# A two-layer decoder trunk: attention in calls of four heads, the first block's scores as one matmul over both key parts, sinks as a column behind the scores, the division on VectorE

## Chip, cores and metric

One core of a Trainium2 chip. The time is device microseconds of one execution, the median of three: 1176.08 us for the kernel before (1176.0 to 1176.14). Five engines work in it, each through its own queue in order: TensorE (PE in the profile; PEld its weight loads), VectorE (DVE), ScalarE (ACT), GpSimd (POOL) and SyncE (SP), which here only issues DMAs.

## What is computed

Two layers on 256 rows of 1024 floats. A layer is a half-step SwiGLU FFN, a mixing sub-layer and a second FFN, each with RMS norms before and behind it. The change lies in one branch of the mixing sub-layer, attention over a sliding window:

```python
def sliding_window_attention(q, k, v, sinks):
    # 16 query heads of 64, 2 key heads; blocks of 128 rows; a block sees itself and the one before
    scores = jnp.einsum('bnqgrd,bnkgd->bngrqk', qb, k2) * scale
    scores = jnp.where(valid[None, :, None, None], scores, MASK_VALUE)
    m = jnp.maximum(scores.max(axis=-1), sink)
    p = jnp.exp(scores - m[..., None])
    probs = p / (p.sum(axis=-1) + jnp.exp(sink - m))[..., None]
    out = jnp.einsum('bngrqk,bnkgd->bnqgrd', probs, v2)
```

The first block of 128 rows has nothing before it, so its scores have 128 columns; the second block's have 256. The sink is one more logit per head: it enters the maximum and the sum, and has no value.

The mixing sub-layer has a second branch (a gated unit, "gating"), two sigmoid gates and an output projection.

## The kernel before

**Precision.** Each fp32 operand is split into a high and a low part that the matmul unit takes at its faster fp32 rate: ScalarE casts the high part (`high`, L143, for weights; L206 for activations), VectorE subtracts to get the low part (L152, L207). A product is then three matmuls: high by high, high by low, low by high. For the scores the query's two parts are kept stacked, so two matmuls do: one with the keys' high part (`kth`, L766), one with their low part (`ktl`, L767).

**Weights.** They stream from HBM in units of 512 KB through four raw buffers and nine split buffers. After the product of a unit the program splits further units up to seven ahead (`AHEAD`, in `upto`).

**Order.** The program fixes the order of every engine's queue itself (`manual_schedule`); the framework puts in the waits that data and reused buffers need. In the middle of the mixing sub-layer TensorE goes through 48 products, one per weight unit: 8 for the gated unit's input (0 to 7), 8 for the queries (8 to 15), then the gate b (16 to 23), the gated unit's branch (24 to 31), the gate a (32 to 39) and the attention's branch (40 to 47). `beside` runs each product and puts other work ahead of it and behind it. A place is a half-step: 2c is ahead of product c, 2c + 1 behind it; 2c + 1 and 2c + 2 follow each other with no product between, only the split of the next weight unit.

**Attention** (`attend`) is a generator that is resumed at half-steps counted from its start: scores on TensorE at 0; at +3 VectorE adds the mask, takes the maximum with the sink as starting value (one instruction per head, L773), and negates it (L777); at +4 ScalarE exponentiates each head with that bias and sums the row (L786); at +7 VectorE takes the reciprocal of the sum plus the sink's exponential (L779, L788, L791, L793) and GpSimd multiplies (L794); at +11 TensorE transposes the probabilities (L803), ScalarE and VectorE split them; at +16 the value products (L815, L816); at +18 to +21 ScalarE copies one half of the partitions over (L826), VectorE adds the two halves ("sides", L829), and the result is split (L832, L834). `ATTEND` holds the half-steps at which the calls start. There are six calls per layer: for each key head, all eight heads of the first block in one call, then the second block in two calls of four heads.

**What else is at those places.** Query evacuations (L917, L920) up to product 16, copies of finished gate products (L935), and at product 31 the sigmoid of gate b on ScalarE (L945), for which ScalarE loads another table, and its product on GpSimd (L948).

**Buffers.** TensorE's results go to eight PSUM banks in turn (`mm`); the 512-wide temporaries to six buffers (`t2`), the probabilities to two (`t4`). Which buffer is given next, and so whom the next writer waits for, is fixed when the program is built.

Of the kernel before, what the change touches and what calls it, by code (L numbers as in the profile page):

```python
# [30 lines left out]
NKV = 2  # L31
HD = 64
# [21 lines left out]

WARM = (11, 6)

ATTEND = (27, 32, 38, 44, 50, 56)
GATING = (9, 10, 11, 12)

GATE = (31, 33)  # L60
# [3 lines left out]
def trunk(ctx: ExitStack, tc: tile.TileContext, a: dict, out: bass.AP):  # L64
    nc = tc.nc

    def pool(name, bufs, **kw):
        return ctx.enter_context(tc.tile_pool(name=name, bufs=bufs, **kw))

    const = pool("const", 1)  # L70
# [5 lines left out]
    t4 = pool("t4", 2)  # L76
    t2 = pool("t2", 6)
    kvp = pool("kv", 1)
# [3 lines left out]
    tiny2 = pool("tiny2", 2)  # L82
# [122 lines left out]
    def split(h, lo, src):  # L205
        nc.scalar.copy(h, src)  # L206
        nc.vector.tensor_tensor(out=lo, in0=src, in1=f(h), op=ALU.subtract)  # L207
# [40 lines left out]
    def bank():  # L248
        return new(mm, [P, 512], "mm")
# [401 lines left out]
    class FFN:  # L651
# [10 lines left out]
        def prepare(self):  # L662
            self.into = [(new(m8, [P, 8, S], "m8", F32R), new(m8, [P, 8, S], "m8", F32R))]
# [27 lines left out]
    class Mix:  # L691
# [29 lines left out]
        def prepare(self):  # L721
            vs = new(n8, [P, NT, D], "n8")
            vv = new(kvp, [P, NT, NKV, 2, HD], "vv", F32R)
            kth = new(kvp, [P, NKV, S], "kth", F32R)
# [25 lines left out]
        def attend(self, g, n, heads):  # L750


            _, vv, kth, ktl = self.into[:4]
            l, qs_, yah, yal = self.l, self.qs, self.yah, self.yal
            nh = len(heads)
            order = heads[0::2] + heads[1::2]
            nk = (n + 1) * P
            qs = rows_of(n)
            half = nh // 2
            s = [bank().rearrange("p (a b) -> p a b", a=half) for _ in range(2)]  # L760
            for i in range(half):
                for r in range(2):


                    q_ = qs_[r][:, heads[0] // 2 + i, qs]
                    nc.tensor.matmul(s[r][:, i, :], q_, kth[:, g, 0:nk], start=True, stop=False)  # L766
                    nc.tensor.matmul(s[r][:, i, :], q_, ktl[r][:, g, 0:nk], start=False, stop=True)  # L767
            yield 3
            m = new(tiny2, [P, 8], "m")
            p = new(t4, [P, nh, nk], "t4")  # L770
            mk = mask.rearrange("p a b -> p (a b)")[:, 256 - nk:]
            for i, hd in enumerate(order):
                nc.vector.tensor_tensor_reduce(out=p[:, i, :], in0=s[i // half][:, i % half, :], in1=mk, scale=1.0,  # L773
                                               scalar=sinks[:, l, hd:hd + 1], op0=ALU.add, op1=ALU.max,
                                               accum_out=m[:, i:i + 1])
            nm = new(tiny2, [P, 8], "nm")
            nc.vector.tensor_scalar(out=nm[:, :nh], in0=m[:, :nh], scalar1=-1.0, scalar2=None, op0=ALU.mult)  # L777
            sk = new(tiny2, [P, 8], "sk")
# [5 lines left out]
            sm = new(tiny2, [P, 8], "sm")  # L784
            for i in range(nh):
                nc.scalar.activation(p[:, i, :], p[:, i, :], AF.Exp, bias=nm[:, i:i + 1],  # L786
                                     accum_out=sm[:, i:i + 1])
            nc.scalar.activation(sk[:, :nh], sk[:, :nh], AF.Exp)  # L788
            yield 3
            dn = new(tiny2, [P, 8], "dn")  # L790
            nc.vector.tensor_tensor(out=dn[:, :nh], in0=sm[:, :nh], in1=sk[:, :nh], op=ALU.add)  # L791
            rd = new(tiny2, [P, 8], "rd")
            nc.vector.reciprocal(rd[:, :nh], dn[:, :nh])  # L793
            nc.gpsimd.tensor_tensor(out=p, in0=p, in1=rd[:, :nh].unsqueeze(2).to_broadcast([P, nh, nk]),  # L794
                                    op=ALU.mult)
            yield 4
            parts = []
            for i0 in range(0, nh, 4):

                for c in range(n + 1):  # L800
                    ps = bank()
                    for i, hd in enumerate(range(i0, i0 + 4)):
                        nc.tensor.transpose(ps[:, i * P:(i + 1) * P], p[:, hd, c * P:(c + 1) * P], ident)  # L803
                    ph, pl = new(t2, [P, 512], "t2", F32R), new(t2, [P, 512], "t2", F32R)
                    split(ph, pl, ps)
                    parts.append((i0, c, ph, pl))
            yield 5
            outs = []
            for i0, c, ph, pl in parts:
                if c == 0:  # L810
                    o = bank()
                    outs.append((i0, o.rearrange("p (a b) -> p a b", a=4)))

                v = vv[:, c, g].rearrange("p r d -> p (r d)")
                nc.tensor.matmul(o, v, ph, start=(c == 0), stop=False)  # L815
                nc.tensor.matmul(o, v, pl, start=False, stop=(c == n))  # L816
            yield 2

            y0, y = [new(t2, [P, half, P], "t2") for _ in range(2)]
            sides = []  # L820
            for r in range(2):
                i0, o = outs[r % len(outs)]
                at = r * half - i0
                sides.append((slice(r * HD, (r + 1) * HD), slice((1 - r) * HD, (2 - r) * HD), o[:, at:at + half, :]))
            for own, other, o in sides:
                nc.scalar.copy(y0[own], o[other])  # L826
            yield 1
            for own, other, o in sides:
                nc.vector.tensor_tensor(out=y[own], in0=o[own], in1=y0[own], op=ALU.add)  # L829
            yield 1  # L830
            js = slice(heads[0] // 2, heads[0] // 2 + half)
            nc.scalar.copy(yah[:, js, qs], y)  # L832
            yield 1
            nc.vector.tensor_tensor(out=yal[:, js, qs], in0=y, in1=f(yah[:, js, qs]), op=ALU.subtract)  # L834

        def middle(self, xt, xth, xtl, turn1, early):
# [86 lines left out]
            calls = []  # L923
            for g in range(NKV):
                h0 = g * 8
                calls.append((g, 0, list(range(h0, h0 + 8))))
                for i0 in range(0, 8, 4):
                    calls.append((g, 1, list(range(h0 + i0, h0 + i0 + 4))))
# [63 lines left out]
    ident = new(const, [P, P], "ident")  # L992
# [20 lines left out]
    sinks = new(const, [P, DEPTH, NH], "sinks")  # L1013
# [3 lines left out]
    mask = new(const, [P, 2, P], "mask")  # L1017
# [4 lines left out]
                            base=0, pattern=[[-1, P]], channel_multiplier=1)  # L1022


    ktl = [new(const, [P, NKV, S], f"ktl{r}", F32R) for r in range(2)]
    for k in ktl:
        nc.gpsimd.memset(f(k), 0.0)

# [44 lines left out]
    parts = [new(tiny2, [P, 2], "parts") for _ in range(NT)]  # L1073
# [38 lines left out]
    for i in range(4):  # L1112
# [3 lines left out]
                            in1=g0[:, 4:8].unsqueeze(2).to_broadcast([P, 4, P]), op=ALU.mult)  # L1116
# [129 lines left out]
```

## Time and profile before

| | |
|---|---|
| median of 3 runs | 1176.08 us |
| the profiled execution | 1175.91 us, its span 1174.0 us |
| granted TensorE clock | 0.999 |
| PE, DVE, ACT, POOL busy | 99%, 72%, 58%, 5% of the span |
| GpSimd's divisions (L794) | 12, 26.1 us |
| scores of the first block (L766, L767, 128 columns) | 64 matmuls |

A row of the order of time has start, duration, engine, line, operation, output and inputs, their shapes, and in brackets how long the engine was idle before and who ended that. Durations of matmuls are latencies and overlap; what one costs TensorE is the distance to the next start. A row of the waits has who waited for whom, the total in us, how often, and the longest. A row of the groups has the number of instructions, busy us and mean ns, then idle time ahead of them. A row of the stretches has its bounds, its length, busy us of PE, PEld, DVE, ACT and POOL, then clock, DMA share and GB/s.

### The profile page before, as it was taken

The page shows a single profiled execution, that of the slowest core. Times are in us where ns is not written, and L with a number is a line of the kernel's source. Part 1 is how long each engine was busy: PE and PEld are TensorE (multiplying, and loading weights), DVE is VectorE, ACT ScalarE, POOL GpSimd, SP SyncE. Part 2 cuts the span into 40 slices and gives each one's busy share as a digit, 9 for nine tenths or more (in the row PEclk, how much of TensorE's full clock was granted, in tenths as well). Part 3 has the DMA queues.
Part 4 walks back from the last instruction along what each step waited for, and adds up shares of the span by engine and source line. Part 5 has one row for each costly group of instructions (what it writes and reads, how often), then busy time and mean ns, then how long its engine had stood idle before and what let it go on. Part 6 is the DMA issues. An engine that isn't in the chain of part 4 may idle for free.

```text
span 1174.0 us, 16947 instructions
## 1 busy us (share of the span) xinstructions
PE 1164.8 (99%) x6293; PEld 1006.9 (86%) x6293; DVE 842.6 (72%) x1430; ACT 675.4 (58%) x1147; POOL 58.9 (5%) x43
## 2 busy tenths in 40 slices
PE   9999999999999999999999999999999999999997
PEld 7888888999888888888888888889988888888886
DVE  6767758877787867766676677589778787676752
ACT  6656644657775456555455665455577754555551
POOL 0000000001131000000000000000021220000000
PEclk9999999999999999999999999999999999999999
DMA  7576673645457346557635657745544662565560
GB/s 249 182 255 230 219 250 141 203 168 175 140 175 241 137 142 215 183 198 266 216 108 193 224 193 240 230 141 183 182 169 137 210 225 81 179 200 198 198 210 37
DMA packets 61427, 220.81 MB, mean 188 GB/s; under 512 B 7072, under 2 KB 7072, under 8 KB 61344
## 3 DMA queue, kind: packets, MB, share of 16 engines
q1 hardware_dynamic: 61056, 219.46, 56.1%
q8 instruction: 50, 0.82, 0.3%
q10 hardware_dynamic: 288, 0.27, 0.1%
q14 instruction: 33, 0.27, 0.1%
HBM read 218.65 MB, written 1.05 MB: 187 GB/s over the span
## 4 chain that ended last, share of the span: by engine, by line
PE 99%; ACT 0%; DVE 0%; issue 0%; DVEq 0%; POOL 0%; POOLq 0%
PE mm L289 51%; PE mm L319 34%; PE mm L296 3%; PE mm L297 3%; PE mm L298 3%; PE mm L254 1%; PE mm L803 1%; PE mm L767 1%; PE mm L766 1%; PE mm L736 1%; PE mm L816 0%; PE mm L815 0%; PE mm L1065 0%; PE mm L276 0%; ACT n L1038 0%; ACT t L1113 0%
## 5 line engine op out<-in xcount | busy, mean ns | idle before, releaser
L152 DVE TENSOR_TENSOR wl<-raw,wh 128x1024 fp32r<-128x1024 f32 x370 | 452.7, 1248 | 88.0 <-ACT wh L143 85.9
L143 ACT CAST wh<-raw 128x1024 fp32r<-128x1024 f32 x370 | 381.7, 1052 | 152.9 <-DMA raw<-in_ffn_w 71.4
L289 PE MATMUL mm<-wh,m 128*128 128x512 f32 x1088 | 341.7, 391 | 0.0
L319 PE MATMUL mm<-xt,wh 128*128 128x512 f32 x1152 | 276.6, 391 | 0.0
L319 PEld LDWEIGHTS mm<-xt,wh 128*128 128x128 f32 x1152 | 211.4, 188 | 40.7
L289 PEld LDWEIGHTS mm<-wh,m 128*128 128x128 f32 x1088 | 204.3, 188 | 42.1
L289 PE MATMUL mm<-wl,m 128*128 128x512 f32 x544 | 211.8, 389 | 0.0
L319 PEld LDWEIGHTS mm<-xt,wl 128*128 128x128 f32 x1152 | 147.7, 191 | 5.6
L319 PE MATMUL mm<-xt,wl 128*128 128x256 f32 x1152 | 149.4, 283 | 0.0
L289 PE MATMUL mm<-wh,xt 128*128 128x512 f32 (+1 forms) x480 | 144.1, 378 | 0.0
L681 DVE TENSOR_TENSOR t<-mm,t 128x256 f32<-128x256 f32 x144 | 61.0, 424 | 101.7 <-ACT t L680 101.7
L289 PEld LDWEIGHTS mm<-wl,m 128*128 128x128 f32 x544 | 102.2, 188 | 20.6
L680 ACT COPY t<-mm 128x256 f32<-128x256 f32 x144 | 52.4, 364 | 88.7 <-PE mm L319 88.7
L289 PEld LDWEIGHTS mm<-wh,xt 128*128 128x128 f32 x480 | 88.4, 188 | 16.0
L289 PE MATMUL mm<-wl,xt 128*128 128x512 f32 (+1 forms) x240 | 87.5, 375 | 0.0
L296 PE MATMUL mm<-xt,wh 128*128 128x256 f32 x256 | 73.3, 286 | 0.0
L298 PE MATMUL mm<-xt,wl 128*128 128x256 f32 x256 | 72.4, 283 | 0.0
L297 PE MATMUL mm<-xt,wh 128*128 128x256 f32 x256 | 72.4, 283 | 0.0
L683 ACT ACTIVATE t<-t 128x256 f32<-128x256 f32 x72 | 30.1, 418 | 46.3 <-DVE t L681 46.3
L289 PE MATMUL mm<-m,xt 128*128 128x512 f32 x216 | 54.5, 397 | 0.0
L289 PEld LDWEIGHTS mm<-wl,xt 128*128 128x128 f32 x240 | 45.2, 188 | 7.9
L794 POOL TENSOR_TENSOR t<-t,rd 128x1024 f32<-128x1024 f32 x12 | 26.1, 2171 | 505.8 <-DVE rd L793 488.2
(156 smaller groups left out, 1094.0 us busy)
## 6 DMA issues: line engine op xcount, KB each, us to landing
raw<-in_ffn_w SPq DMA_DIRECT2D x263, 512.0 KB, 4.5
raw<-in_w_in SPq DMA_DIRECT2D x84, 512.0 KB, 4.1
raw<-in_w_sgu_branch SPq DMA_DIRECT2D x16, 512.0 KB, 3.6
raw<-in_w_attn_branch SPq DMA_DIRECT2D x16, 512.0 KB, 3.8
raw<-in_w_out SPq DMA_DIRECT2D x16, 512.0 KB, 4.5
gain<-in_ffn_post_g SPq DMA_DIRECT2D x4, 512.0 KB, 6.4
gain<-in_ffn_pre_g SPq DMA_DIRECT2D x3, 512.0 KB, 6.7
x<-in_x SPq DMA_DIRECT2D x4, 256.0 KB, 4.9
```

Of the source, the lines that this page charges most:

```text
L143: nc.scalar.copy(h, self.raw[u])
L152: nc.vector.tensor_tensor(out=lo, in0=self.raw[u], in1=f(h), op=ALU.subtract)
L254: nc.tensor.transpose(ps[:, k, :], src[:, (c0 + k) * P:(c0 + k + 1) * P], ident)
L289: nc.tensor.matmul(o, every[i][0], every[i][1], start=start and i == 0, stop=stop and i == 2)
L296: nc.tensor.matmul(o, wh[:, ks], ah[:, k, :], start=(k == 0), stop=False)
L297: nc.tensor.matmul(o, wh[:, ks], al[:, k, :], start=False, stop=False)
L298: nc.tensor.matmul(o, wl[:, ks], ah[:, k, :], start=False, stop=(k == KD - 1))
L319: nc.tensor.matmul(out_, w[:, k * P:(k + 1) * P], x, start=(k == 0 and x.shape[1] == 2 * S), stop=(k == KD - 1 and x.shape[1] == 2 * S))
L680: nc.scalar.copy(y[:, half, :], o[half][:, S:2 * S])
L681: nc.vector.tensor_tensor(out=y[:, half, :], in0=o[half][:, 0:S], in1=y[:, half, :], op=ALU.add)
L683: nc.scalar.activation(y[:, 0, :], y[:, 0, :], AF.Silu)
L794: nc.gpsimd.tensor_tensor(out=p, in0=p, in1=rd[:, :nh].unsqueeze(2).to_broadcast([P, nh, nk]), op=ALU.mult)
```

## The change

Attention is called eight times per layer with four heads each, for both blocks. In the first block one matmul of 256 columns goes over the keys' low and high part side by side (`keys`, three planes: low part for the query's upper half, high part, low part for the other half; any two neighbours are one operand); VectorE first adds the mask to one half of the result (L775), and the reduction adds the other half (L779). The sink is copied as one more column behind the scores (L785), so that the exponential's row sum holds it; the small additions and exponentials for it go. VectorE multiplies by the reciprocal (L795) in GpSimd's place. The offsets inside a call stay; the calls start at other half-steps.

```diff
-ATTEND = (27, 32, 38, 44, 50, 56)
+ATTEND = (25, 29, 33, 38, 43, 47, 52, 57)
...
-            s = [bank().rearrange("p (a b) -> p a b", a=half) for _ in range(2)]
-            for i in range(half):
+            s = [bank().rearrange("p (a b) -> p a b", a=2) for _ in range(2)]
+            for i in range(2):
                 for r in range(2):
...
                     q_ = qs_[r][:, heads[0] // 2 + i, qs]
-                    nc.tensor.matmul(s[r][:, i, :], q_, kth[:, g, 0:nk], start=True, stop=False)
-                    nc.tensor.matmul(s[r][:, i, :], q_, ktl[r][:, g, 0:nk], start=False, stop=True)
+                    if n == 0:
+                        nc.tensor.matmul(s[r][:, i, :], q_, keys[:, r:r + 2, g, 0:nk], start=True, stop=True)
+                    else:
+                        nc.tensor.matmul(s[r][:, i, :], q_, kth[:, g, 0:nk], start=True, stop=False)
+                        nc.tensor.matmul(s[r][:, i, :], q_, ktl[r][:, g, 0:nk], start=False, stop=True)
             yield 3
...
+            p = new(t4, [P, 4, nk + 1], "t4")
+            if n == 0:
+                for r in range(2):
+                    nc.vector.tensor_tensor(out=p[:, 2 * r:2 * r + 2, 0:nk], in0=s[r][:, :, 0:nk],
+                                            in1=mask[:, 1:2, :].to_broadcast([P, 2, P]), op=ALU.add)
...
-            nc.vector.tensor_tensor(
-                out=sk[:, :nh].rearrange("p (r j) -> p r j", r=2),
-                in0=sinks[:, l, heads[0]:heads[0] + nh].rearrange("p (j r) -> p r j", r=2),
-                in1=nm[:, :nh].rearrange("p (r j) -> p r j", r=2), op=ALU.add)
+            nc.scalar.copy(p[:, :, nk:nk + 1].rearrange("p (r j) a -> p r (j a)", r=2),
+                           sinks[:, l, heads[0]:heads[0] + 4].rearrange("p (j r) -> p r j", r=2))
             yield 1
...
-            nc.scalar.activation(sk[:, :nh], sk[:, :nh], AF.Exp)
             yield 3
-            nc.vector.tensor_tensor(out=dn[:, :nh], in0=sm[:, :nh], in1=sk[:, :nh], op=ALU.add)
-            nc.vector.reciprocal(rd[:, :nh], dn[:, :nh])
-            nc.gpsimd.tensor_tensor(out=p, in0=p, in1=rd[:, :nh].unsqueeze(2).to_broadcast([P, nh, nk]),
-                                    op=ALU.mult)
+            nc.vector.reciprocal(rd, sm)
+            nc.vector.tensor_tensor(out=p[:, :, 0:nk], in0=p[:, :, 0:nk],
+                                    in1=rd.unsqueeze(2).to_broadcast([P, 4, nk]), op=ALU.mult)
             yield 4
...
+            calls = [(g, n, list(range(h, h + 4))) for g in range(NKV) for n in range(NT)
+                     for h in range(g * 8, g * 8 + 8, 4)]
...
+    keys = new(const, [P, 3, NKV, S], "keys", F32R)
+    kth, ktl = keys[:, 1], (keys[:, 0], keys[:, 2])
```

The calls of a layer are numbered here in the order in which they start: before, 1 and 4 are the eight-head calls; after, 1, 2, 5 and 6 are calls of the first block, 3, 4, 7 and 8 of the second.

VectorE's queue in the first layer, before, from the split of the second call's probabilities to the first call's sides and the next call's reduction (t_592, t_595: that split; wl: a weight's low part; t_604: the sides; mm_3141: scores of the fourth call):

```order
L207 TENSOR_TENSOR t_592_3123<-mm_3117,t_591_3122 128x512
L207 TENSOR_TENSOR t_595_3132<-mm_3126,t_594_3131 128x512
L152 TENSOR_TENSOR wl_3088<-raw_2980,wh_3087 128x1024
L791 TENSOR_TENSOR dn_3171<-sm_3093,sk_3084 128x4
L793 RECIPROCAL rd_3173<-dn_3171 128x4
L152 TENSOR_TENSOR wl_3136<-raw_3004,wh_3135 128x1024
L829 TENSOR_TENSOR t_604_3177<-mm_3111,t_603_3176 64x512
L829 TENSOR_TENSOR t_604_3177<-mm_3114,t_603_3176 64x512
L773 ISA t_609_3201,m_3200<-mm_3141,mask_125,sinks_122 128x128
```

The same place after: the split of call 3 (t_598, t_601), call 1's sides (t_592), call 4's reciprocal and division (t_583), and call 5's mask additions and first reduction (t_608):

```order
L207 TENSOR_TENSOR t_598_3131<-mm_3125,t_597_3130 128x512
L207 TENSOR_TENSOR t_601_3140<-mm_3134,t_600_3139 128x512
L823 TENSOR_TENSOR t_592_3116<-mm_3073,t_591_3115 64x256 x2
L794 RECIPROCAL rd_3160<-sm_3092 128x4
L795 TENSOR_TENSOR t_583_3077<-t_583_3077,rd_3160 128x4x256
L152 TENSOR_TENSOR wl_3120<-raw_3012,wh_3119 128x1024
L775 TENSOR_TENSOR t_608_3171<-mm_3109,mask_125 128x2x128
L775 TENSOR_TENSOR t_608_3171<-mm_3110,mask_125 128x2x128
L779 ISA t_608_3171,m_3170<-mm_3109,t_608_3171,sinks_122 128x128
```

Behind these rows come three more reductions, the negation, a small low part (L828), a weight's low part and call 2's sides (L823). By the wait counts of the built program the second split waits for call 2's first value product (its buffer), and TensorE's transposes of call 4 wait for call 2's sides (their bank).

ScalarE's queue, before, at the last call's exponentials (t_668) and the sigmoid (n_542), with the split of the fifth call's probabilities (t_678, t_681) ahead of the table load:

```order
L786 ACTIVATE t_668_3451,sm_3473<-t_668_3451,nm_3456 128x256 x4
L788 ACTIVATE sk_3458<-sk_3458 128x4
L206 CAST t_678_3496<-mm_3491 128x512
L206 CAST t_681_3505<-mm_3500 128x512
L143 CAST wh_3509<-raw_3392 128x1024
L945 ACT_TABLE_LOAD
L945 ACTIVATE n_542_2914<-n_542_2914 128x2x512
```

After: call 8's exponentials (t_676), the sigmoid (n_541), and then the split of call 7's probabilities (t_686, t_689):

```order
L790 ACTIVATE t_676_3461,sm_3485<-t_676_3461,nm_3466 128x257 x4
L143 CAST wh_3490<-raw_3380 128x1024
L935 ACT_TABLE_LOAD
L935 ACTIVATE n_541_2898<-n_541_2898 128x2x512
L206 CAST t_686_3519<-mm_3514 128x512
L206 CAST t_689_3528<-mm_3523 128x512
```

The casts of the seventh call now stand behind the table load and the sigmoid; before, the casts of the last call but one stood ahead of them.

More of the change, by code (lines that the diff above doesn't have):

```diff
@@ L772, in attend @@
+            yield 3
+            m = new(tiny2, [P, 4], "m")
+            p = new(t4, [P, 4, nk + 1], "t4")
[3 more added lines that the diff above has]
+                                            in1=mask[:, 1:2, :].to_broadcast([P, 2, P]), op=ALU.add)
             for i, hd in enumerate(order):
-                nc.vector.tensor_tensor_reduce(out=p[:, i, :], in0=s[i // half][:, i % half, :], in1=mk, scale=1.0,
-                                               scalar=sinks[:, l, hd:hd + 1], op0=ALU.add, op1=ALU.max,
+                part = s[i // 2][:, i % 2, :]
+                nc.vector.tensor_tensor_reduce(out=p[:, i, 0:nk], in0=part[:, P:2 * P] if n == 0 else part,
+                                               in1=p[:, i, 0:nk] if n == 0 else mask.rearrange("p a b -> p (a b)"),
+                                               scale=1.0, scalar=sinks[:, l, hd:hd + 1], op0=ALU.add, op1=ALU.max,
@@ L775, in attend @@
                                                accum_out=m[:, i:i + 1])
[L776 to L782 removed]
+            nm = new(tiny2, [P, 4], "nm")
@@ L783, in attend @@
+            nc.vector.tensor_scalar(out=nm, in0=m, scalar1=-1.0, scalar2=None, op0=ALU.mult)
+            nc.scalar.copy(p[:, :, nk:nk + 1].rearrange("p (r j) a -> p r (j a)", r=2),
+                           sinks[:, l, heads[0]:heads[0] + 4].rearrange("p (j r) -> p r j", r=2))
             yield 1
-            sm = new(tiny2, [P, 8], "sm")
-            for i in range(nh):
+            sm = new(tiny2, [P, 4], "sm")
+            for i in range(4):
                 nc.scalar.activation(p[:, i, :], p[:, i, :], AF.Exp, bias=nm[:, i:i + 1],
@@ L807, in attend @@
-            yield 5
[L808 to L812, printed above, removed]
+            for c in range(n + 1):
+                ps = bank()
+                for i in range(4):
+                    nc.tensor.transpose(ps[:, i * P:(i + 1) * P], p[:, i, c * P:(c + 1) * P], ident)
+                ph, pl = new(t2, [P, 512], "t2", F32R), new(t2, [P, 512], "t2", F32R)
+                split(ph, pl, ps)
+                parts.append((c, ph, pl))
@@ L814, in attend @@
+            yield 5
+            o = bank()
+            for c, ph, pl in parts:
                 v = vv[:, c, g].rearrange("p r d -> p (r d)")
@@ L816, in attend @@
                 nc.tensor.matmul(o, v, pl, start=False, stop=(c == n))
+            o = o.rearrange("p (a b) -> p a b", a=4)
             yield 2
[L819 to L824, printed above, removed]
+            y0, y = [new(t2, [P, 2, P], "t2") for _ in range(2)]
+            sides = [(slice(r * HD, (r + 1) * HD), slice((1 - r) * HD, (2 - r) * HD), o[:, 2 * r:2 * r + 2, :])
+                     for r in range(2)]
             for own, other, o in sides:
@@ L830, in attend @@
             yield 1
-            js = slice(heads[0] // 2, heads[0] // 2 + half)
+            js = slice(heads[0] // 2, heads[0] // 2 + 2)
             nc.scalar.copy(yah[:, js, qs], y)
```

24 lines of the change are left out of this document (1 added, 23 removed).

## The prediction

> **What bounds the kernel now.** I read the page's busy times and its chain, then the waits of TensorE (PE), then the busy times by stretch.
>
> ```profile
> span 1174.0 us, 16947 instructions
> PE 1164.8 (99%) x6293; PEld 1006.9 (86%) x6293; DVE 842.6 (72%) x1430; ACT 675.4 (58%) x1147; POOL 58.9 (5%) x43
> PE 99%; ACT 0%; DVE 0%; issue 0%; DVEq 0%; POOL 0%; POOLq 0%
> ```
> ```profile
> PE mm L1065 <- POOL ident masks.py:199: 1.4, 1, 1.4
> PE mm L289 <- ACT n L1038: 0.4, 1, 0.4
> ```
> ```profile
> 306.00:320.00 14.00, 14.00 (x79) 12.07 (x79) 10.56 (x23) 10.98 (x29) 1.90 (x1) 1.00 0.44 136
> ```
>
> The chain that ended last is TensorE alone; its two longest waits of the whole run, shown here, are 1.4 and 0.4 us and lie at the start. In the stretch of the attention that the third view shows, TensorE is busy for 14.00 of 14 us, VectorE for 10.56 and ScalarE for 10.98. So a microsecond taken from TensorE's work is a microsecond of the kernel, and a microsecond that TensorE must wait is one as well. Work on VectorE costs nothing until TensorE reaches something VectorE hasn't finished. Two questions decide: how much matmul time goes, and whether VectorE and ScalarE still keep ahead.
>
> **What TensorE saves.** These are matmuls in order of time; the first column is the start, and what counts is start to start, since each is shown with its latency.
>
> ```profile
> 267.08 0.22 PE L766 MATMUL mm<-kth,m 128*128 128x128 f32 x1
> ...
> 268.82 0.33 PE L296 MATMUL mm<-xt,wh 128*128 128x256 f32 x1
> 268.99 0.28 PE L297 MATMUL mm<-xt,wh 128*128 128x256 f32 x1
> ...
> 274.63 0.28 PE L766 MATMUL mm<-kth,m 128*128 128x256 f32 x1
> ...
> 275.59 0.40 PE L289 MATMUL mm<-wh,xt 128*128 128x512 f32 x1
> ...
> 283.78 0.28 PE L766 MATMUL mm<-kth,m 128*128 128x256 f32 x1
> 284.73 1.03 PE L803 MATMUL mm<-ident,t 128*128 128x128 f32 x8
> 285.52 0.48 PE L289 MATMUL mm<-wh,xt 128*128 128x512 f32 x1
> 285.84 0.40 PE L289 MATMUL mm<-wl,xt 128*128 128x512 f32 x1
> ...
> 293.82 0.39 PE L815 MATMUL mm<-t,vv 128*128 128x512 f32 x1
> 294.73 1.03 PE L803 MATMUL mm<-ident,t 128*128 128x128 f32 x8
> ```
>
> The sixteen 128-column score matmuls of a first-block call, with the longer step behind them, take 268.99 - 267.08 - 0.12 = 1.79 us. Eight of 256 columns take 275.59 - 274.63 = 0.96 us. A layer has two such calls of eight heads: (1.79 - 0.96) x 2 x 2 layers = 3.3 us. The eight transposes cost 285.84 - 284.73 - 0.23 = 0.88 us in one group, and two groups of four (0.36 + 0.09 each) cost 0.89: nothing. The value products stay. [...]
>
> Whether a moving operand in two pieces of 128, as the side-by-side keys are, streams like one of 256 no row shows. Between 0.12 us each (the 256-column rows) and 0.22 (two of 128), I take 0.12, the same column count; at the other end the gain is gone.
>
> **What VectorE and ScalarE take on.** The rows that price it, VectorE first, then ScalarE and GpSimd (POOL):
>
> ```profile
> L681 DVE TENSOR_TENSOR t<-mm,t 128x256 f32<-128x256 f32 x144 | 61.0, 424 | 101.7 <-ACT t L680 101.7
> L143 ACT CAST wh<-raw 128x1024 fp32r<-128x1024 f32 x370 | 381.7, 1052 | 152.9 <-DMA raw<-in_ffn_w 71.4
> ```
> ```profile
> 301.17 0.35 DVE L773 CUSTOM_DVE_ANT_0 t<-mm,mask,sinks 128x128 f32<-128x128 f32 x1
> ...
> 303.46 0.17 DVE L777 TENSOR_SCALAR nm<-m 128x8 f32<-128x8 f32 x1
> ...
> 308.01 1.29 DVE L207 TENSOR_TENSOR t<-mm,t 128x512 fp32r<-128x512 f32 x2 [2.43 <-ACT t L206]
> 309.21 1.22 DVE L152 TENSOR_TENSOR wl<-raw,wh 128x1024 fp32r<-128x1024 f32 x1
> 310.35 0.16 DVE L791 TENSOR_TENSOR dn<-sm,sk 128x8 f32<-128x8 f32 x1
> 310.54 0.20 DVE L793 RECIPROCAL rd<-dn 128x8 f32<-128x8 f32 x1
> 310.70 0.86 DVE L829 TENSOR_TENSOR t<-mm,t 64x256 f32<-64x256 f32 x2
> 311.59 2.30 DVE L152 TENSOR_TENSOR wl<-raw,wh 128x1024 fp32r<-128x1024 f32 x1
> 313.92 0.48 DVE L773 CUSTOM_DVE_ANT_0 t<-mm,mask,sinks 128x256 f32<-128x256 f32 x1
> ...
> 315.67 0.17 DVE L777 TENSOR_SCALAR nm<-m 128x4 f32<-128x4 f32 x1
> ...
> 315.95 0.42 DVE L834 TENSOR_TENSOR m<-t,m 128x256 fp32r<-128x256 f32 x1
> 316.29 1.22 DVE L152 TENSOR_TENSOR wl<-raw,wh 128x1024 fp32r<-128x1024 f32 x1
> ```
> ```profile
> 303.73 0.40 ACT L786 ACTIVATE t<-t,nm 128x128 f32<-128x128 f32 x1 [0.98 <-DVE nm L777]
> ...
> 306.83 0.19 ACT L788 ACTIVATE sk<-sk 128x8 f32<-128x8 f32 x1
> ...
> 307.40 1.06 ACT L206 CAST t<-mm 128x512 fp32r<-128x512 f32 x2
> ...
> 315.93 0.51 ACT L786 ACTIVATE t<-t,nm 128x256 f32<-128x256 f32 x1 [2.93 <-DVE nm L777]
> ...
> 317.92 0.19 ACT L788 ACTIVATE sk<-sk 128x4 f32<-128x4 f32 x1
> ...
> 331.11 1.28 ACT L945 ACT_TABLE_LOAD   x1
> 332.41 1.06 ACT L945 ACTIVATE n<-n 128x1024 f32<-128x1024 f32 x1
> ```
> ```profile
> 310.91 1.90 POOL L794 TENSOR_TENSOR t<-t,rd 128x1024 f32<-128x1024 f32 x1 [9.34 <-DVE rd L793]
> ```
>
> Per layer VectorE gets eight additions of the mask (0.34 to 0.42 each, by L834's spacing and L681) and eight divisions: four of 512 elements (0.6, like L207) and four of 1024 (1.14, a weight's low part, 310.35 - 309.21): 3.2 + 2.4 + 4.6 = 10 us. The small additions that go give back some 2 us. GpSimd's division gives back something too: the low part at 311.59 began while GpSimd's division ran, and ended 1.08 us after that one's end at 312.81, 2.30 us instead of 1.22. [...] That saves 1.1 us where they met. ScalarE's copies of the sinks (0.1 to 0.2 each) replace its small exponentials: nothing. No DMA is added or moved.
>
> What matters is that VectorE's and ScalarE's queues are in order, and each call now makes VectorE reduce, ScalarE exponentiate, and VectorE divide, eight times per layer instead of six. I number the calls 1 to 8 (their half-steps: 25, 29, 33, 38, 43, 47, 52, 57) and price two stretches; a product of 12 matmuls is (283.78 - 275.59) / 3 = 2.73 us.
>
> **First wait, at call 4's transposes.** The second half of call 3's split takes the buffer that call 2's value product reads, so VectorE can't start it before that product. From there TensorE has two value matmuls (0.455), a product (2.73), four scores (0.48), a product (2.73) and four value matmuls (0.91), 7.3 us, until call 4's transposes. Their bank is freed by the addition of call 2's sides (L823). In VectorE's queue that stands behind: the value matmul's end (0.39), split (0.6), call 1's sides (0.89), call 4's reciprocal and division (0.2 + 1.14), a low part (1.14), call 5's mask, maximum and negation (0.8 + 1.15 + 0.2 = about 2.1), a small low part (0.34), a low part (1.14), and itself (0.86): 8.8 us. TensorE waits 1.5 us. Its second group of transposes takes a bank freed by a ScalarE copy behind call 5's exponentials: 6.5 (the sum up to the negation) + 1.55 + 1.05 + 0.6 = 9.7, against 8.8 + 0.4: another 0.5. In the profile the sides of the call before were done at 301 us and their bank taken at 306.5; that cover of 5 us is what the closer calls use up.
>
> **Second wait, at call 8's transposes.** From call 4's second group TensorE has nine products (24.6), sixteen scores (1.92), 0.45 + 0.45 + 0.45 + 0.88 of transposes and 0.91 + 0.455 + 0.455 + 0.91 of value products: 31.4 us. VectorE starts 0.6 later and has six splits (3.6), eight low parts (9.1), one reduction of call 6 (2.1), two of 256 columns (1.92 each), two short and two long divisions (4.4), three small low parts (1.0) and three sums of sides (2.6): 26.7 us. It also waits for ScalarE: 0.8 at call 5's split, 1.5 at call 6's, and 3.9 at call 7's, where the cast stands behind call 8's exponentials (1.99), a weight cast (1.05), the table load (1.28) and the sigmoid (1.0), plus its own 0.6, while VectorE has 2.0 to do. That is 33.5 us, so TensorE waits 2.0.
>
> **The sum.** 4.0 us per layer, both layers being laid out alike: 8.0. The profiled execution took 1175.91 us, its span and 1.9 around it, 0.17 under the median of 1176.08. 1175.9 - 3.3 + 8.0 = 1180.6; with the 0.2 to the median, 1180.8 us. The sums of durations carry about a twentieth: 0.45 of the first stretch and 1.7 of the second, 4.3 us over both layers, so 1176.5 to 1185.
>
> **Rivals.** *VectorE keeps ahead, faster.* If an instruction starts before the one ahead has written (as 309.21 to 310.35 shows, less than its 1.22) more often than I reckon, and the ScalarE waits overlap, both stretches shrink. The point is the first one: at 7.3 us or less there, and 6% off the second, TensorE never waits and the time is 1172.8. For it: VectorE had 3.4 of 14 us free. Against: the order of the queue leaves it no other work to put ahead. *The gain is just eaten.* One of the two stretches is short and the other fits: 1176.1 - 3.3 + 4 = 1176.8, no change. *Worse.* The sigmoid's end lets GpSimd's gate product run into the low part or division ahead of call 8's transposes, and these wait as at 311.59: 1.1 more per layer, 1183.0; with the twentieth on top, over 1185. *The scores don't do what they say*: pieces of 128 at 0.22 us, no gain, 1184; I count it with the last one.
>
> **How the numbers follow.** Forecast 0.57, VectorE ahead 0.15, gain just eaten 0.18, worse 0.10. A measurement of this kernel tells about 0.2%, 2.4 us, from no change. Faster by more holds the first rival and a sliver: 0.16. Within it lie the second rival and the forecast's low edge: 0.22. Slower: 0.62. The range leaves out the worst tenth: 1172.6 to 1185.0; the forecast's own is 1176.5 to 1185.
>
> **What would show it.** L764 at 0.12 us start to start, 32 of them, shows the gain. Among TensorE's waits, new rows for L802 and L289 with VectorE (L823, L779, L795) as releasers, some 4 us per layer, show the loss; with no such rows the second and third steps are wrong. VectorE's wait for the cast behind the sigmoid (L207 on L206, about 4 us) shows the second stretch. The forecast is wrong if TensorE's idle time stays at 2 us, or if its waits fall at products for lack of weights (L152), which I hold to be seven units ahead.

## The result, and the profile after

The changed kernel takes 1186.54 us (median of 5 executions, 1185.36 to 1186.88) against 1176.08 for the kernel before: a ratio of 1.0087, 95% interval 1.0076 to 1.0097. It is slower, as forecast, but by 10.5 us and not by 4.7, and 1186.54 lies above the range (1172.6 to 1185.0). The profiled execution took 1186.32 us.

The page of the changed kernel, its span, its busy times and the shares of the chain that ended last:

```profile
span 1184.3 us, 16899 instructions
PE 1165.6 (98%) x6261; PEld 1003.8 (85%) x6261; DVE 855.2 (72%) x1458; ACT 676.1 (57%) x1163; POOL 33.1 (3%) x31
PE 80%; DVE 11%; ACT 6%; issue 1%; DMA 1%; DVEq 0%; POOL 0%; ACTq 0%; POOLq 0%
```

TensorE was the whole chain before; now VectorE and ScalarE hold 17% of it. TensorE's waits name the places:

```profile
PE mm L802 <- DVE t L795: 5.2, 2, 2.6
PE mm L289 <- DVE m L779: 1.8, 2, 1.0
...
PE mm L802 <- DVE t L823: 1.0, 2, 0.5
PE mm L254 <- DVE t L502: 0.9, 1, 0.9
...
PE mm L802 <- ACT n L925: 0.4, 2, 0.2
```

Four of these rows are the attention's, 8.4 us over both layers; the kernel before has none there. Call 8's transposes wait for their division (L795). A product ahead of call 4's transposes waits for call 5's reduction (L779), and these transposes then wait for call 2's sides (L823) and for a copy on ScalarE (L925). The row for L254 lies in the first FFN.

The stretches of the first layer's attention (length, then PE, PEld, DVE, ACT, POOL, the granted clock, DMA share, GB/s):

```profile
306.00:320.00 14.00, 13.32 (x69) 10.78 (x67) 11.58 (x27) 12.00 (x33) 0.00 (x0) 1.00 0.41 131
...
334.00:348.00 14.00, 11.40 (x48) 9.16 (x47) 9.38 (x13) 12.56 (x21) 6.41 (x4) 0.88 0.40 117
```

VectorE is not full in either, 11.58 and 9.38 of 14 us. So TensorE waits for an order of work and not for VectorE's throughput, which the last experiments test. The second row shows something else, a clock of 0.88. TensorE in order of time: the merged scores, the first wait, the second, and what follows it:

```profile
265.32 0.64 PE L764 MATMUL mm<-keys,m 128*128 128x256 f32 x4
265.80 0.28 PE L296 MATMUL mm<-xt,wh 128*128 128x256 f32 x1
...
303.66 0.39 PE L289 MATMUL mm<-wh,m 128*128 128x512 f32 x1
304.82 0.50 PE L289 MATMUL mm<-wh,m 128*128 128x512 f32 x1 [0.77 <-DVE m L779]
...
307.03 0.39 PE L812 MATMUL mm<-t,vv 128*128 128x512 f32 x1
307.88 0.63 PE L802 MATMUL mm<-ident,t 128*128 128x128 f32 x4 [0.47 <-DVE t L823]
308.73 0.44 PE L802 MATMUL mm<-ident,t 128*128 128x128 f32 x2 [0.21 <-ACT n L925]
...
340.06 0.40 PE L812 MATMUL mm<-t,vv 128*128 128x512 f32 x1
343.05 1.31 PE L802 MATMUL mm<-ident,t 128*128 128x128 f32 x8 [2.60 <-DVE t L795]
344.01 0.78 PE L289 MATMUL mm<-wh,xt 128*128 128x512 f32 x1
344.58 0.63 PE L289 MATMUL mm<-wl,xt 128*128 128x512 f32 x1
345.01 1.05 PE L289 MATMUL mm<-wh,xt 128*128 128x512 f32 x2
345.86 0.63 PE L289 MATMUL mm<-wl,xt 128*128 128x512 f32 x1
...
347.38 0.62 PE L289 MATMUL mm<-wh,xt 128*128 128x512 f32 x2
```

Four merged score matmuls take 265.80 - 265.32 = 0.48 us, 0.12 each. A 512-column matmul's start is usually 0.23 us ahead of the next one's. So the first wait cost 304.82 - 303.66 - 0.23 = 0.93 us, then 307.88 - 307.03 - 0.23 = 0.62, and 0.4 behind the first four transposes: some 1.9 us. The second cost 343.05 - 340.06 - 0.23 = 2.76. Behind it the matmuls start 345.01 - 344.58 = 0.43 us apart, half speed, until about 347. The second layer has the same waits, the last from 925.12 to 928.11 (start to start, as in 340.06 to 343.05), but its matmuls go on at 0.23.

What VectorE, GpSimd and ScalarE did meanwhile:

```profile
338.34 1.29 DVE L207 TENSOR_TENSOR t<-mm,t 128x512 fp32r<-128x512 f32 x2 [4.09 <-ACT t L206]
339.55 2.01 DVE L152 TENSOR_TENSOR wl<-raw,wh 128x1024 fp32r<-128x1024 f32 x1
341.48 0.17 DVE L794 RECIPROCAL rd<-sm 128x4 f32<-128x4 f32 x1
341.68 1.23 DVE L795 TENSOR_TENSOR t<-t,rd 128x1024 f32<-128x1024 f32 x1
```
```profile
337.92 2.56 POOL L938 TENSOR_TENSOR n<-n,n 128x512 f32<-128x512 f32 x2 [266.45 <-ACT n L935]
```
```profile
335.48 1.28 ACT L935 ACT_TABLE_LOAD   x1
336.78 1.06 ACT L935 ACTIVATE n<-n 128x1024 f32<-128x1024 f32 x1
337.74 1.06 ACT L206 CAST t<-mm 128x512 fp32r<-128x512 f32 x2
```

VectorE stood still for 4.09 us, as the prediction had it (about 4), until ScalarE had loaded its table, made the sigmoid and cast call 7's probabilities. Then its low part took 2.01 us where others take 1.22, since GpSimd's gate product ran until 340.48.

### The profile page after: what moved, and what is told of

It reads as the page before. It is cut to its first block, busy times and chain, and to the rows that moved or that the text cites. A ratio compares the mean times of both kernels' runs of the same rounds, so it can differ in the third digit from the quotient of the medians.

```text
span 1184.3 us, 16899 instructions
## 1 busy us (share of the span) xinstructions
PE 1165.6 (98%) x6261; PEld 1003.8 (85%) x6261; DVE 855.2 (72%) x1458; ACT 676.1 (57%) x1163; POOL 33.1 (3%) x31
## 4 chain that ended last, share of the span: by engine, by line
PE 80%; DVE 11%; ACT 6%; issue 1%; DMA 1%; DVEq 0%; POOL 0%; ACTq 0%; POOLq 0%
PE mm L289 40%; PE mm L319 33%; DVE wl L152 3%; ACT t L790 2%; ACT wh L143 2%; DVE t L779 2%; PE mm L297 2%; PE mm L296 2%; PE mm L298 2%; PE mm L254 1%; DVE t L207 1%; DVE t L795 1%; DVE m L914 1%; ACT t L206 1%; DVE t L775 0%
## 5 line engine op out<-in xcount | busy, mean ns | idle before, releaser
L319 PEld LDWEIGHTS mm<-xt,wh 128*128 128x128 f32 x1152 | 211.4, 188 | 41.2 <-ACT t L363 0.6
L289 PE MATMUL mm<-wh,xt 128*128 128x512 f32 (+1 forms) x480 | 147.2, 382 | 0.0
L297 PEld LDWEIGHTS mm<-xt,wh 128*128 128x128 f32 x256 | 49.1, 192 | 0.0
```

What stands on the lines that cost most here:

```text
L289: nc.tensor.matmul(o, every[i][0], every[i][1], start=start and i == 0, stop=stop and i == 2)
L297: nc.tensor.matmul(o, wh[:, ks], al[:, k, :], start=False, stop=False)
L319: nc.tensor.matmul(out_, w[:, k * P:(k + 1) * P], x, start=(k == 0 and x.shape[1] == 2 * S), stop=(k == KD - 1 and x.shape[1] == 2 * S))
```

## Experiments

Each was timed beside the kernel before, whose median was 1176.1 to 1176.2 throughout.

**The gate later.** The second wait should hang on the sigmoid's place.

```diff
-GATE = (31, 33)
+GATE = (33, 35)
```

> The gate's two sigmoids, with their table load and GpSimd's product, come two products later (GATE 33 and 35 for 31 and 33); all else is as in the changed kernel. Theory of the two waits with the clock: call 7's cast no longer stands behind the table load and the sigmoid, so the wait at call 8's transposes (2.77 us in layer 0, 2.76 in layer 1) falls below 0.5 us, the matmuls behind it in layer 0 run at 0.23 us again (some 2 us there), and the first wait stays (L779, L823, L925, 1.9 to 2.2 us per layer): 1186.5 - 5 - 2 = 1179.5 us. Rival, VectorE's own work alone is too much between call 4 and call 8: only the overlap with GpSimd's product goes, 0.8 per layer, 1185 us. A third, the wait but not the clock hangs on the gap: 1181.5 us with matmuls of 0.43 us still in layer 0.

1178.21 us (1177.61 to 1178.91), ratio 1.0017 (1.0008 to 1.0026). In its waits of TensorE the row for L795 is gone and the other three stand as they did:

```profile
PE mm L289 <- DVE m L779: 1.8, 2, 1.0
...
PE mm L802 <- DVE t L823: 1.0, 2, 0.5
...
PE mm L802 <- ACT n L925: 0.4, 2, 0.2
```

8.3 us come back for two numbers. VectorE has the same instructions between call 4 and call 8, but it now waits 1.73 us for call 7's cast where it waited 4.09. The rival (1185) falls, and so does the third (1181.5). The time is 1.3 below the 1179.5 of the theory. The two profiled executions, 1186.32 and 1178.65, lie 7.7 us apart: 5.5 for the second wait in both layers, 1.6 for the slow matmuls (worked out below), and the rest lies ahead of any changed work.

**The gate product later in the program.**

```diff
-                yield 2
+                yield 6
                 for t in range(NT):
                     nc.gpsimd.tensor_tensor(out=so[:, t, b], in0=so[:, t, b], in1=gb[:, t, b], op=ALU.mult)
```

> Only GpSimd's gate product comes later (two products later, 6 half-steps behind the sigmoid for 2); the sigmoid and the table load stay where they are. Theory: the low part ahead of call 8's division takes 1.2 us instead of 2.0, since no GpSimd instruction runs beside it, and the second wait falls from 2.8 to 2.0 us, the predicted size, in both layers: 1.6 us. If the gap's length decides about the clock, 2.2 us of gap is short enough and the slow matmuls in layer 0 go too: 1186.5 - 1.6 - 2 = 1183 us. Rival, the low part was long for another reason: its row stays at 2.0 us and the time at 1186.5.

1183.98 us (1183.53 to 1186.62). The edit delayed nothing: GpSimd's queue holds nothing else there, and the product still began at 336.42, as soon as the sigmoid was done (335.28 and 1.06 us). The gap is as long as before:

```profile
336.42 2.56 POOL L938 TENSOR_TENSOR n<-n,n 128x512 f32<-128x512 f32 x2 [267.07 <-ACT n L935]
```
```profile
338.59 0.40 PE L812 MATMUL mm<-t,vv 128*128 128x512 f32 x1
341.56 1.06 PE L802 MATMUL mm<-ident,t 128*128 128x128 f32 x8 [2.57 <-DVE t L795]
342.38 0.48 PE L289 MATMUL mm<-wh,xt 128*128 128x512 f32 x1
342.70 0.40 PE L289 MATMUL mm<-wl,xt 128*128 128x512 f32 x1
342.93 0.63 PE L289 MATMUL mm<-wh,xt 128*128 128x512 f32 x2
```

As a test of the low part it says nothing. But it is the changed kernel once more, and this time the clock held: 0.23 us from start to start right behind a gap of 2.97. So a gap of 3.0 us brings the slow clock in some cases and not in others. Three of its five executions took 1183.5 to 1184.0 us with a mean granted clock of 0.998, and the one with 0.996 took 1186.62; the fifth, 1185.86 with 0.998, is not explained by the clock.

**The gate product really later.** GpSimd first copies four numbers out of call 8's divided probabilities.

```diff
+            if n == 1 and heads[0] == 12:
+                gw = new(tiny2, [P, 4], "gw")
+                nc.gpsimd.tensor_copy(out=gw, in_=p[:, :, 0])
...
-                yield 2
+                yield 6
```

> Moving GpSimd's gate product in the program did not move it on the chip, since nothing stood ahead of it in GpSimd's queue. Here GpSimd first copies four numbers of call 8's divided probabilities (one small added instruction, whose result is not used), so that its gate product starts behind that division. Sigmoid and table load stay. Theory: the low part ahead of the division takes 1.2 us, as it does elsewhere, for 2.0, and the wait at call 8's transposes falls from 2.8 to 2.0 us in both layers, 1.6 us together: 1182.3 us against 1183.9 where the clock holds; and with 2.0 us of gap no run falls below a mean clock of 0.998. Rival, the low part stays at 2.0 us with GpSimd idle: no gain, 1183.9 us or more.

1182.21 us (1181.39 to 1183.21), every execution with a mean clock of 0.999. VectorE's low part, and TensorE's transposes:

```profile
337.86 1.22 DVE L152 TENSOR_TENSOR wl<-raw,wh 128x1024 fp32r<-128x1024 f32 x1
```
```profile
338.36 0.40 PE L815 MATMUL mm<-t,vv 128*128 128x512 f32 x1
340.57 1.07 PE L805 MATMUL mm<-ident,t 128*128 128x128 f32 x8 [1.81 <-DVE t L795]
```

1.22 us with GpSimd idle, and a wait of 2.21 - 0.23 = 1.98 us, the size predicted. So 2.76 - 1.98 = 0.8 us of the second wait is GpSimd's product beside the low part.

**The gap filled.** The same wait, but TensorE is kept busy in it.

```diff
                 ps = bank()
+                if n == 1 and c == 0 and heads[0] == 12:
+                    for _ in range(10):
+                        nc.tensor.matmul(ps, keys[:, 1, 0, 0:P], keys[:, 0:2, 0, :], start=True, stop=True)
```

> Ahead of call 8's first transpose TensorE gets ten matmuls of 512 columns, 2.3 us, into the bank that the transposes then overwrite; the output does not change. They fill most of the gap of 2.8 us and move nothing else. Theory that the empty gap costs the clock: the matmuls behind it run at 0.23 us in layer 0 as well, and the kernel, with more work, gets faster: 1186.5 - 2 = 1184.5 us. Rival, the clock falls for another reason, or by chance: 1186.5 us or a little above, with matmuls of 0.43 us in layer 0 again.

1183.44 us (1183.37 to 1185.04), ratio 1.0067 (1.0053 to 1.0080): with 20 matmuls more it takes no longer than the same work without them (1183.98, above). All five executions show 0.998 or 0.999. The filling, the transposes and what follows:

```profile
338.96 2.43 PE L803 MATMUL mm<-keys 128*128 128x512 f32 x10
341.66 1.09 PE L805 MATMUL mm<-ident,t 128*128 128x128 f32 x8 [0.27 <-DVE t L795]
342.50 0.47 PE L289 MATMUL mm<-wh,xt 128*128 128x512 f32 x1
342.82 0.39 PE L289 MATMUL mm<-wl,xt 128*128 128x512 f32 x1
```

No slow matmul, and the transposes come no earlier (341.66, against 341.56 in the same work without the filling). Alone this could be chance, since the clock held there too without any filling; the next two settle it.

**The gap longer**, by one and by two passes of VectorE ahead of call 8's division.

```diff
             nc.vector.reciprocal(rd, sm)
+            if n == 1 and heads[0] == 12:
+                nc.vector.tensor_tensor(out=p[:, :, 0:nk], in0=p[:, :, 0:nk], in1=p[:, :, 0:nk], op=ALU.max)
```

> The changed kernel with one more pass of VectorE over call 8's probabilities ahead of their division (the maximum of each with itself, 1024 elements, 1.14 us, which changes no value). The gap ahead of call 8's transposes grows from 2.8 to 3.9 us in both layers. Without a slow clock the time is 1183.9 + 2.3 = 1186.2 us. Theory that the length of the gap decides about the clock behind it: now it falls in every run and in both layers, 2 us each: 1190 us, no run with a mean clock over 0.997. Rival, chance alone: half of the runs at 1186.2, the others 2 us above.

> The same with two more passes: a gap of 5.1 us, 1183.9 + 4.6 = 1188.5 us without a slow clock. Theory of the gap's length: slow behind each gap in every run, 1192.5 us; a price that grows with the gap would show here as more than 2 us per gap. Rival, chance alone: 1188.5 us in half of the runs, 1190.5 in the others.

1189.51 us (1188.52 to 1191.44, 4 executions) and 1195.22 (1194.96 to 1195.58). The mean clocks are 0.992 to 0.995 in every execution of both. With one pass, the stretch behind the gap in the first layer, then in the second:

```profile
342.00:346.00 4.00, 3.41 (x13) 3.06 (x14) 4.00 (x3) 0.24 (x1) 2.68 (x2) 0.62 0.22 90
```
```profile
930.00:934.00 4.00, 4.00 (x12) 3.15 (x11) 3.95 (x5) 0.87 (x2) 1.24 (x1) 0.57 0.06 25
```

Clocks of 0.62 and 0.57: both layers now pay. The gap, from the last value product to the transposes, grew to 4.1 us (338.48 to 342.59), which makes 1183.9 + 2 x (4.1 - 3.0) = 1186.1 at full clock; the other 3.4 us are 1.7 for each gap. With two passes I had reckoned a gap of 5.1; it became 6.35, since the division then ran beside GpSimd's second gate product (2.19 us for 1.23). That makes 1183.9 + 2 x 3.35 = 1190.6, and 2.3 for each gap. Chance alone falls: over 4 us the clock dropped in all nine executions, at some 2 us a gap.

**Who divides.** GpSimd again, all else as changed.

```diff
-            nc.vector.tensor_tensor(out=p[:, :, 0:nk], in0=p[:, :, 0:nk],
+            nc.gpsimd.tensor_tensor(out=p[:, :, 0:nk], in0=p[:, :, 0:nk],
```

> GpSimd multiplies by the reciprocal again, as in the kernel before; calls, merged scores and sink column stay. Theory of the two waits: call 4's division (1.14 us) goes out of VectorE's queue ahead of call 5's reductions and call 2's sides, so the first wait falls from 1.9 to 2.2 us per layer to 0.5 to 1.0 (the sides, L823, or the copy, L925). The second wait does not get shorter, since there ScalarE's cast behind the sigmoid is late and GpSimd now has the gate product ahead of call 8's division: some 2.8 us, released by L795 on POOL. Together 1186.5 - 2.5 = 1184 us, range 1182.5 to 1185. Rival, the division on VectorE is what costs: eight of them, 7 us per layer, of which the wait of 4.7 us per layer would go: 1177 us.

1181.23 us (1179.33 to 1182.76), below the range. The base was wrong: I had reckoned from 1186.5, which holds a slow clock, where 1183.9 - 2.5 = 1181.4. The rival (1177) falls. The wait for the reduction (L779) went; what is left:

```profile
PE mm L802 <- POOL t L795: 4.5, 2, 2.3
...
PE mm L802 <- ACT n L925: 0.4, 2, 0.2
PE mm L802 <- DVE t L823: 0.4, 2, 0.2
```

The second wait stays with either engine dividing, since both get their input late. GpSimd's gate product was not ahead of this division, as I had expected, but behind it, and the low part took 1.22 us here too. The clock is seen here as well: executions with a mean of 0.999 took 1179.33 and 1180.15 us, those with 0.995 to 0.997 took 1181.23 to 1182.76, by gaps of 2.6 to 2.7 us. The same edit the other way, VectorE dividing in the kernel before:

```diff
-            nc.gpsimd.tensor_tensor(out=p, in0=p, in1=rd[:, :nh].unsqueeze(2).to_broadcast([P, nh, nk]),
+            nc.vector.tensor_tensor(out=p, in0=p, in1=rd[:, :nh].unsqueeze(2).to_broadcast([P, nh, nk]),
```

> The kernel before with one part of the change alone: VectorE multiplies by the reciprocal, in calls of eight and four heads at the old starts. Theory: VectorE has 3.4 us of 14 free there and the calls stand further apart, so the added 1.14 us per call stay under TensorE's work but for a wait of at most 1 us per layer: 1176.2 to 1178.2 us. Rival, the division on VectorE is by itself the costly part of the change: 1180 us or more.

1178.81 us (1178.28 to 1179.69), ratio 1.0022 (1.0014 to 1.0031), 0.6 over what I gave it. One new wait, at the fifth call's scores (308.49 in the first layer), behind a copy in ScalarE's queue:

```profile
PE mm L766 <- ACT n L935: 1.9, 2, 1.0
```

So the division on VectorE has a price in the order before too, 2.7 us, though far from the whole 10 us, and the rival (1180 or more) falls.

**The merge behind waits.** The first block's scores in two matmuls again, at the changed starts.

```diff
-                    if n == 0:
-                        nc.tensor.matmul(s[r][:, i, :], q_, keys[:, r:r + 2, g, 0:nk], start=True, stop=True)
-                    else:
-                        nc.tensor.matmul(s[r][:, i, :], q_, kth[:, g, 0:nk], start=True, stop=False)
-                        nc.tensor.matmul(s[r][:, i, :], q_, ktl[r][:, g, 0:nk], start=False, stop=True)
+                    nc.tensor.matmul(s[r][:, i, 0:nk], q_, kth[:, g, 0:nk], start=True, stop=False)
+                    nc.tensor.matmul(s[r][:, i, 0:nk], q_, ktl[r][:, g, 0:nk], start=False, stop=True)
```

(the mask's additions go with it)

> The changed kernel at its own starts, but with the scores of the first block as two matmuls of 128 columns each and no extra addition of the mask; all else stays. Theory: the score matmuls cost TensorE 1.64 us more per layer, and this same 1.64 with 0.8 us less for VectorE (two mask additions of 0.38 less per call of the first block) comes out of the first wait; the second stays. Net about nothing: 1184 to 1187 us against the changed kernel's 1186.5, or 1183.9 where its clock holds. Rival, the merge's 3.3 us are there whether TensorE waits or not: 1189.8 us, or 1187.2 where the clock holds.

1183.12 us (1182.68 to 1184.93), below the 1184 to 1187 that I gave it. Taking out an edit that saves TensorE 3.3 us makes this kernel no slower. The waits gave it back, the second one too (line numbers are 10 lower here, and the row for the reduction is gone):

```profile
PE mm L792 <- DVE t L785: 3.8, 2, 1.9
...
PE mm L792 <- DVE t L813: 0.7, 2, 0.4
...
PE mm L792 <- ACT n L915: 0.4, 2, 0.2
```

I had not counted that the scores of calls 5 and 6, 0.4 us each, lie between call 4's transposes and call 8's: TensorE comes later by that much.

**The starts alone.** All the work of the change, other starts.

```diff
-ATTEND = (25, 29, 33, 38, 43, 47, 52, 57)
+ATTEND = (25, 29, 34, 40, 45, 49, 54, 58)
```

> The changed kernel with nothing but other starts of the calls: ATTEND = 25, 29, 34, 40, 45, 49, 54, 58. Work and instructions are the same. Theory of the two waits: with 5 to 6 half-steps between the calls that collide, the split of call 3 no longer has call 4's and call 5's work close behind it, and call 7's cast no longer stands behind the sigmoid; TensorE then has no wait over 0.3 us in the attention, and what is left is the gain: 1176.1 - 3.3 = 1172.8 us, range 1172 to 1174.5. Rival, VectorE's added 10 us per layer cannot be hidden wherever they stand: waits of 2 us or more per layer remain, 1177 us or more.

1173.69 us (1173.19 to 1174.16, 11 executions), ratio to the kernel before 0.9979 (0.9970 to 0.9988): faster than both. The same stretches as above:

```profile
306.00:320.00 14.00, 14.00 (x74) 11.83 (x74) 12.47 (x31) 11.35 (x32) 0.00 (x0) 1.00 0.46 140
...
334.00:348.00 14.00, 14.00 (x68) 11.64 (x67) 12.57 (x20) 13.85 (x23) 3.01 (x2) 1.00 0.55 181
```

TensorE is busy for 14.00 of 14 us in both. VectorE has more to do in each than in the changed kernel and keeps ahead. The rival falls: the 12.9 us between the two kernels hang on the starts of six calls.

**Spread, without the merge** (the edit shown above, at these starts).

> The spread calls again, but the first block's scores are two matmuls of 128 columns each, as in the kernel before, and VectorE adds the mask within the reduction; sink column and division stay. Theory: nothing waits in either kernel, so the difference to the spread kernel with merged scores is TensorE's gain alone, 3.3 us: 1176.1 us, as the kernel before. Rival, two pieces of 128 do not stream like 256 columns, or the merge's gain is something else: a difference under 1.5 us.

1176.61 us (1176.31 to 1177.46), ratio 1.0006 (0.9997 to 1.0015). The merge is worth 2.9 us by the medians, and 3.3 by the spans of the profiled executions (1175.5 and 1172.2). The two-piece operand streams like 256 columns, 0.12 us each.

**Spread, GpSimd dividing.**

> The spread starts (25, 29, 34, 40, 45, 49, 54, 58) with the division on GpSimd. Theory: where TensorE waits for nothing, the engine that divides does not matter: 1173.7 us as with VectorE, within 0.6. Rival, GpSimd's slower division (1.9 us for 1.14) and the low parts that it holds up bring a wait back: 1175.5 us or more.

1173.32 us (1172.79 to 1174.11, 9 executions), ratio 0.9976 (0.9967 to 0.9986). Within 0.4 of VectorE: with no wait, it does not matter who divides.

## Why the prediction was wrong

The direction and the two waits came as forecast. Two steps failed: the size of the second wait (2.0 us per layer, measured 2.76), and the step that "a microsecond that TensorE must wait is one as well", which left out what a wait does to the clock (1.6 us in the profiled execution).

*TensorE saves 3.3 us.* Right: 0.12 us per matmul in the trace, 2.9 to 3.3 us in the pair of spread kernels.

*First wait, 2.0 us per layer.* Right in size, 1.9 in the first layer and 2.2 in the second (1.2, 0.65, 0.4 by the same reckoning). Its largest part came earlier than I placed it: the product ahead of call 4's transposes needs a bank that call 5's reduction (L779) frees; I had looked for the bank of the transposes alone. The sum did not change by that, since the reductions stand in the same queue ahead of call 2's sides: 0.93 + 0.62 is the 1.5 that I gave the sides.

*Second wait, 2.0 us per layer.* This step failed in size: 2.76. The 3.9 us of ScalarE were right (4.09), but I took a low part behind them at its usual price and set GpSimd's product beside it aside as the rival "worse", with 1.1 us and one chance in ten. Without that product the term holds, 1.98 in the run that held it back. That the product runs there follows from the forecast's own step: the sigmoid that delays the cast also lets GpSimd's product go, so the two meet here unless something holds the product back. The trace tells two instructions apart there: the two splits at 338.34, each with one input in a PSUM bank, took 1.29 us beside the product, as the two at 308.01 in the kernel before did with GpSimd idle; the low part, with no input there, took 2.01 us for 1.22.

*Left out: the clock.* I took a wait to cost its length, and gave no reason for it. In the profiled execution the gap of 3.0 us also cost, in the first layer, 3.37 us for eight matmuls (344.01 to 347.38) that took 1.94 in the run where the clock held, 1.4 us, and 0.1 at the transposes: 1.6. Four of the changed kernel's five executions have mean clocks of 0.996 or 0.997.

*The sum, redone* against the profiled execution: 1175.9 - 3.3 + 4.1 (first wait) + 5.5 (second) + 1.6 (clock) = 1183.8. The wait of 0.9 at L254, some 192 us into the run, is ahead of any changed work; it varies between kernels that are alike up to there (0.4 with the gate later, none with the gap filled), so it is no part of the change. Behind it the matmuls stand 1.1 us later against the kernel before, which makes 1184.9; 1.4 of 1186.3 stay unnamed, about equally in both layers. The spread kernel without the merge, which waits for nothing in the attention, loses some 0.3 us per layer there against the kernel before, so about half of it is there without any wait; no row names it. Of the 5.7 us between the forecast for this execution (1180.6) and 1186.3, the second wait is 1.5, the clock 1.6, the first wait 0.1, and for 2.5 no run shows a cause in the change.

*The rivals.* "VectorE keeps ahead" was wrong for these starts, and its price, 1172.8, is what the spread starts nearly give (1173.7): the mechanism stood, its condition was the order. "The gain is just eaten" needed one wait to stay away, and both came. "The scores don't do what they say" is refuted. "Worse" came true in the second wait, at 0.8 us per layer for 1.1. Neither it nor the clock alone took the time past the range: 1180.8 + 0.1 + 1.5 + 1.6 = 1184.0 lies inside, and the 2.5 us without a shown cause did the rest.

## What to carry to other kernels

When work moves onto an engine with room, price the order of its queue and not its busy share: the same instructions gave 1186.5 and 1173.7 us with other starts. Follow each late result one engine further, to what the same event sets free (here a sigmoid held back a cast and let GpSimd run into the next step). And a wait on TensorE can cost more than its length: near 3 us it cost 1.6 us more in one layer and nothing in the other, and over 4 us some 2 us more each time.

## What the runs showed of the hardware

A gap of TensorE of 3.0 us from start to start halved the speed of the matmuls behind it in one layer and not in the other. A gap of 4.1 us did so in both (clocks of 0.62 from 342 to 346 and 0.57 from 930 to 934). With 6.35 us the clock was 0.50 from 344 to 348 in the first layer; in the second it fell within the gap (0.83 from 930 to 934, where TensorE did nothing). In the first layer full speed was back 3.3 to 4.1 us after the first transposes. At 2.6 to 3.0 us 8 of 15 executions show a mean clock of 0.997 or less, at 2.2 to 2.3 one of ten, and in the kernels with no gap over 1.5 us none. The mark is a rough one: a single slow stretch lowers the mean by 3.4 x 0.5 / 1184 = 0.0014, and kernels without gaps show 0.998 or 0.999.

What the price hangs on shows in the length of the drop. In the changed kernel, in slices of 0.1 us, the clock is 0.50 from 343.73 to 347.14, 3.41 us (an edge is placed within its slice by the slice's mean). For the kernels with one and two passes more the length is an estimate from the mean clock of longer stretches, taking it as 0.50 or 1.00 throughout. With one pass more, 0.83 from 341 to 344 and 0.70 from 344 to 348 make 3.4 us, up to 346.40, and 0.57 from 930 to 934 makes 3.4 us in the second layer. With two passes, 0.69 from 341 to 344, 0.50 from 344 to 348 and 0.88 from 348 to 352 make 6.8 us, from 342.14 to 348.96: twice as long. A stretch of 3.41 us at half speed can cost 1.7 us; 1.6 was measured in the changed kernel and 1.7 with one pass more. With two passes the first part of the first layer's drop fell into the gap and cost nothing; 3.3 us were left behind it (345.65 to 348.96), 1.7 us at half speed, where the medians give 2.3 for a gap.

The idle time ahead of the slow matmuls was 2.60 us, by the row at 343.05. One of 2.57 us, by the row at 341.56 with the gate product later in the program, and one of 2.59 us in the changed kernel's second layer (928.11) brought no drop. What decides between them no run shows.
